# A feature-major final norm for 704 of 1056 tokens, a re-dealt tail, and three empty jobs behind each key block

## The chip, the core and the metric

The kernel runs as one program on one core of a Trainium2 chip. The core has five engines that run side by side, each through its own instructions in order: TensorE (PE in the profile, with its weight loads as PEld), VectorE (DVE), ScalarE (ACT), GpSimd (POOL) and SyncE (SP), which here only issues DMA transfers. ACT issues a few transfers too. Engines wait for each other through semaphores. The metric is the device time of one execution in microseconds (us); the kernel before takes 1604.93 us, the median of three runs from 1604.6 to 1605.01 us.

## What is computed

The reference is one layer of a streaming encoder, for a prompt of 1024 tokens and a sample of 32 tokens, 1024 features each, all in float32:

```
h  = rmsnorm(x, g_mix) * (1 + sc1) + sh1;   u = h @ w_in         # 8 heads of attention, 4 heads of an mLSTM, gates
ya = chunk-band softmax attention(q, k, v);  ym = mLSTM(...)
x  = x + gt1 * ((sigmoid(ga) * (ya @ w_br_att) + sigmoid(gm) * (ym @ w_br_mlstm)) @ w_out)
h2 = rmsnorm(x, g_ffn) * (1 + sc2) + sh2;   g, up = split(h2 @ w_gate_up)
x  = x + gt2 * ((silu(g) * up) @ w_down)
y  = x * rsqrt(mean(x * x over the 1024 features) + 1e-6) * g_final      # the final norm
```

Results are y for both streams, and the new keys, values, convolution rows and mLSTM states. The change touches the last line, and the order of some work near the first product.

## The kernel before

**Layout.** Prompt and sample are handled as one sequence of 1056 tokens in three tiles of 352 (`TILES`). Activations lie with features on the 128 partitions and tokens along the free dimension: `x2[j]` holds features 128 j to 128 j + 127 of all tokens, j from 0 to 7. Each float32 product is made of three matmuls of rounded operands (high by high, low by high, high by low: `PASSES`), so weights and activations are split into a high and a low part, by ACT (copy, L413) and DVE or POOL (subtraction, L414). `unit` (L447) makes one output block of 128 features by 352 tokens: 8 steps of k with three matmuls each. A product goes into a PSUM bank; the three banks of the pool `mm` go round among units and transposes, and a bank is free when ACT and DVE have taken its content.

**The order of the work.** PE, ACT, DVE and POOL run their instructions in the order in which the Python program emits them; SP's transfers are placed by the tile framework. Two queues of side work are woven in: `side.later` is a list of small jobs, of which `unit` runs one after each of the steps k = 2, 4, 6 (`side.flush(1)`, L450), and generators in `side.jobs` are advanced by `side.tick()`, one tick in two steps of k. An entry `lambda: None` in the list uses up one of these places.

**The start.** The first key block (hp = 0) and value block are computed together in `first_units`, while the input is still being normed. `k_block.run` then evicts the key block from PSUM (ACT L557 and L560, DVE L562), splits the next weights if there is room (L413, L414) and sends the keys out; `v_block.run` evicts the values (ACT L590) and appends `v_tail(0)`, nothing, `v_tail(1)`, nothing, `v_sample` and `cache_kv` to the list. `v_tail` transposes four blocks of values on PE (L615), splits them (ACT L603, DVE L606), and the second one sends them out from ACT's queue (L579, L580). Then `q_block(0)` makes three units with these jobs inside them and evicts each (ACT L643, L646). After it comes the key block of hp = 1 (`mm_868` in the rows below, with the weights `wsp_704`). The other three key blocks are followed by a value block of three units of its own, and at those places the list is empty.

**The end.** The down projection's first 704 tokens (`cut`) are finished in the tiles `cs[j]`. The last loop (from L2211) makes the product of the remaining 352 tokens: for each j, 22 steps of k with three matmuls (L2220), so 66 matmuls and 11 ticks, and adds it to `x2[j]` (DVE L2230). Beside it runs the generator `finish_some`, 15 steps in 75 ticks: eight steps that add `cs[j]` to `x2[j]` (DVE L2192), and then, for six blocks of up to 128 tokens, `Finish`: eight transposes on PE to have tokens on partitions (L2124), the sum of squares by ACT with an accumulator (L2125), three small operations on POOL for the reciprocal root (L2132 to L2134), two multiplications on DVE (L2140) and the output (SP L2144). `End` does the same for the last 352 tokens in three blocks of 128, 128 and 96: `ahead` during the last j, and `last` after it: three transposes (L2162), three squares (L2163), POOL's sum and power per block (L2179, L2180), then per block ACT scales the left half (L2183), DVE the right one (L2184), and ACT's and SP's queues send them (L2188). The block of 96 lies across the end of the prompt, so each of its halves goes out as two transfers.

## Time and profile before

One execution was profiled. Its own time was 1605.1 us, its span, from the first instruction to the last, 1603.4 us; the medians of the runs and this execution agree within 0.2 us. The granted TensorE clock was 0.997 of full speed on the mean.

| what | number |
|---|---|
| median of three runs | 1604.93 us |
| profiled execution: its own time / its span | 1605.1 / 1603.4 us |
| busy: PE, DVE, ACT, POOL | 1574.2, 1133.5, 784.1, 443.0 us |
| idle PE behind one wait in the first 110 us, the longest after the input load | 3.1 us |
| DMA: moved, mean rate | 192.45 MB, 120 GB/s |

How to read it: a group or a row of the timeline gives start, duration, engine, line, operation, output<-inputs, shape and count, and in brackets how long the engine had been idle and what ended it. `PE mm L615 <- ACT t L590: 3.1, 1, 3.1` in a view of waits is: TensorE's instructions of line 615 waited for ACT's of line 590, 3.1 us in total, once, at most 3.1 us. The chain of waits follows the work that ended last back through the program, and gives what each piece added to it.

### The profile page before, as it was taken

The numbers are of one execution on the slowest core, as the hardware profiler recorded it, in microseconds if no ns is written. First come the engines' busy times: TensorE is split into PE (matmuls) and PEld (weight loads), VectorE is DVE, ScalarE is ACT, GpSimd is POOL, SyncE is SP. The second block draws the span as 40 slices with busy tenths as digits, with TensorE's granted clock in tenths as the row PEclk, the third lists the DMA queues.
The fourth block names the chain that finished last, engine by engine and source line by source line (L and its number), as shares of the span: only waits on it lengthen the run. The fifth ranks groups of instructions, "written<-read, shape, count | busy, mean of one in ns | idle before, by whom it ended". The sixth has DMA issues, their size and how long they took to land.

```text
span 1603.4 us, 27301 instructions
## 1 busy us (share of the span) xinstructions
PE 1574.2 (98%) x10229; PEld 1554.3 (97%) x10229; DVE 1133.5 (71%) x2178; ACT 784.1 (49%) x1743; POOL 443.0 (28%) x470
## 2 busy tenths in 40 slices
PE   7899999999999999999999999999999999999997
PEld 7899999999999999999999999999999999999997
DVE  7766564647776855455654699998888986799754
ACT  3556454544455544443443655544544444545443
POOL 1334243434332411000012100565565650000001
PEclk9999999999999999999999999999999999999999
DMA  9822323232223332685353311213222227427454
GB/s 364 262 83 91 100 82 102 89 122 87 67 80 80 72 94 68 120 279 165 122 154 112 107 54 50 97 56 104 81 80 94 67 84 251 135 79 250 135 155 127
DMA packets 209362, 192.45 MB, mean 120 GB/s; under 512 B 11450, under 2 KB 179038, under 8 KB 208206
## 3 DMA queue, kind: packets, MB, share of 16 engines
q1 hardware_dynamic: 206670, 188.87, 37.9%
q8 instruction: 81, 1.33, 0.4%
q10 hardware_dynamic: 2528, 1.77, 0.4%
q14 instruction: 51, 0.42, 0.1%
q0 software_dynamic: 32, 0.06, 0.0%
HBM read 152.19 MB, written 41.63 MB: 121 GB/s over the span
## 4 chain that ended last, share of the span: by engine, by line
PE 89%; DMA 4%; DVE 3%; ACT 2%; issue 1%; SPq 0%; POOL 0%; ACTq 0%; DVEq 0%; POOLq 0%
PE mm L447 41%; PE psb L1817 18%; PE mm L1817 10%; PE mm L2220 3%; PE mm L884 3%; PE psb L2220 2%; PE psV L786 2%; PE psb L2063 2%; DMA xres<-s 1%; PE psS L728 1%; DMA s<-in_w_ada_dram 1%; PE psT L755 1%; PE mm L2063 1%; DMA wraw<-in_w_in_dram 1%; DMA s<-in_x_prompt_dram 1%
## 5 line engine op out<-in xcount | busy, mean ns | idle before, releaser
L447 PE MATMUL mm<-s,wsp 128*128 128x352 f32 x4104 | 687.8, 324 | 0.0
L447 PEld LDWEIGHTS mm<-s,wsp 128*128 128x128 f32 x4104 | 657.1, 188 | 1.5 <-issue 0.4
L414 DVE TENSOR_TENSOR wsp<-wraw,wsp 128x512 fp32r<-128x512 f32 (+1 forms) x280 | 234.9, 855 | 120.3 <-ACT wsp L413 118.7
L1817 PE MATMUL psb<-s,wsp 128*128 128x352 f32 x1611 | 271.7, 322 | 1.5 <-DVE wsp L414 0.8
L413 ACT ACTIVATE wsp<-wraw 128x512 fp32r<-128x512 f32 x336 | 199.4, 617 | 140.7 <-PE psb L1817 45.5
L1817 PEld LDWEIGHTS psb<-s,wsp 128*128 128x128 f32 x1611 | 260.5, 188 | 2.1 <-DVE wsp L414 1.1
L1817 PE MATMUL mm<-s,wsp 128*128 128x352 f32 x933 | 159.3, 322 | 0.0
L1817 PEld LDWEIGHTS mm<-s,wsp 128*128 128x128 f32 x933 | 151.2, 188 | 0.5 <-DVE wsp L414 0.5
L748 POOL TENSOR_SCALAR st<-st,mx 128x640 f32<-128x640 f32 (+5 forms) x72 | 56.1, 779 | 182.6 <-DVE mx L747 168.3
L1207 DVE SCALAR_TENSOR_TENSOR t<-wa,cmix,t 128x512 f32<-128x512 f32 x112 | 89.8, 807 | 14.3 <-DMA wa<-in_w_ada_dram 14.0
L414 POOL TENSOR_TENSOR wsp<-wraw,wsp 128x512 fp32r<-128x512 f32 x56 | 75.1, 1362 | 50.8 <-ACT wsp L413 50.3
L743 ACT ACTIVATE st<-st,mx 128x640 f32<-128x640 f32 (+5 forms) x72 | 47.9, 665 | 67.3 <-DVE mx L742 67.2
L742 DVE CUSTOM_DVE_ANT_0 st<-psS,bias 128x640 f32<-128x640 f32 (+5 forms) x72 | 44.4, 617 | 49.4 <-PE psS L728 35.2
L762 ACT ACTIVATE pT<-psT 128x640 fp32r<-128x640 f32 (+3 forms) x80 | 38.7, 494 | 64.6 <-PE psT L755 51.2
L1764 POOL TENSOR_TENSOR t<-t,sl 128x352 f32<-128x352 f32 x19 | 18.4, 969 | 182.9 <-ACT sl L1762 182.9
L2132 POOL TENSOR_TENSOR fst<-fst 128x1 f32<-128x1 f32 (+1 forms) x6 | 1.2, 194 | 236.6 <-ACT t L2125 236.6
L767 DVE TENSOR_TENSOR pT<-psT,pT 128x640 fp32r<-128x640 f32 (+3 forms) x80 | 44.0, 558 | 22.3 <-ACT pT L762 22.2
L1426 POOL TENSOR_TENSOR wraw<-wraw,raw 128x512 f32<-128x512 f32 x33 | 55.8, 1704 | 0.9
L884 PE MATMUL mm<-s,s 128*128 128x264 f32 (+3 forms) x432 | 54.7, 283 | 0.0
L2220 PE MATMUL mm<-s,wsp 128*128 128x352 f32 x330 | 54.4, 324 | 0.0
L2220 PEld LDWEIGHTS mm<-s,wsp 128*128 128x128 f32 x330 | 53.1, 188 | 0.0
L1426 POOL TENSOR_TENSOR spare<-wraw 128x512 f32<-128x512 f32 x11 | 16.8, 1527 | 130.0 <-DMA wraw<-in_w_gate_up_dram 122.2
(374 smaller groups left out, 2548.0 us busy)
## 6 DMA issues: line engine op xcount, KB each, us to landing
wraw<-in_w_in_dram SPq DMA_DIRECT2D x38, 512.0 KB, 4.3
wraw<-in_w_gate_up_dram SPq DMA_DIRECT2D x33, 512.0 KB, 4.0
wa<-in_w_ada_dram SPq DMA_DIRECT2D x64, 256.0 KB, 2.8
wraw<-in_w_down_dram SPq DMA_DIRECT2D x32, 512.0 KB, 3.7
a_d<-t SPq DMA_DIRECT2D x22, 528.0 KB, 2.7
g_d<-t SPq DMA_DIRECT2D x16, 528.0 KB, 2.7
x<-xres SPq DMA_DIRECT2D x16, 528.0 KB, 6.5
t<-g_d SPq DMA_DIRECT2D x16, 528.0 KB, 4.6
```

The source lines that it names most:

```text
L413: act.activation(dst[:, 0], src, AF.Copy)
L414: eng.tensor_tensor(dst[:, 1], src, f(dst[:, 0]), op=ALU.subtract)
L447: pe.matmul(pt[:, :hi - lo], wt[(w0 + k) // 4][:, a, (w0 + k) % 4], xt[k][:, b, lo:hi], start=(k == 0 and q == 0), stop=(k == n - 1 and q ...
L742: dve.tensor_tensor_reduce(so, sv, bi, -1.0, 3.0e38, ALU.add, ALU.min, mx[:n, 1:2])
L743: act.activation(st[:n, :w], st[:n, :w], AF.Exp, bias=mx[:n, 1:2], scale=-1.0, accum_out=mx[:n, 2:3])
L748: pool.tensor_scalar(st[:n, :w], st[:n, :w], mx[:n, 3:4], 1.0, op0=ALU.mult, op1=ALU.mult)
L884: pe.matmul(pt[:n, :wd], hs[k][:, a, i * P:i * P + n], whl[b][:, k, :wd], start=(k == 0 and q == 0), stop=(k == KD - 1 and q == 2))
L1207: dve.scalar_tensor_tensor(ac[:, c], wa, cmix[:, c, k:k + 1], ac[:, c], op0=ALU.mult, op1=ALU.add)
L1426: self.eng.tensor_tensor(a(dst), a(x), a(y), op=op)
L1817: pe.matmul(acc, wt[:, a, k], x[k][:, b], start=(start and not onto and k == 0 and q == 0), stop=(stop and k == 3 and q == 2), skip_group_ ...
L2063: pe.matmul(acc, wt[k // 4][:, u, k % 4], piece_of[k, i][:, v], start=(k == 0 and q == 0), stop=(k == KP - 1 and q == 2))
L2220: pe.matmul(acc, wt[(k - k0) // 4][:, u, (k - k0) % 4], piece_of[k, 2][:, v], start=(k == 0 and q == 0), stop=(k == NF - 1 and q == 2))
```

## The change

Line numbers of the changed kernel differ by one from L566 on, and by more from L2107 on.

1. `k_block` appends three empty jobs to `side.later`.
2. `finish_some` no longer transposes. Each of its first eight steps adds `cs[j]` to `x2[j]`, squares it on ACT into a tile of 128 by 704, and adds it on POOL to a running tile `known`. After one empty step, six matmuls with a column of ones sum `known` over the partitions into one PSUM tile of 128 by 8, DVE scales it and POOL takes the power for all tokens in one instruction; after three steps more the reciprocal roots are broadcast over the partitions (`bcast_cols`: six transposes on PE, two copies on ACT), and eight steps multiply `x2[j]` in place by `g_final` (a column per j, `gcols`) and by the roots, and send it out. The generator runs with 22 steps in 66 ticks after a delay of 8.
3. The outputs are `y_rows`, feature-major, for the 704 tokens, and `y_end`, token-major, for the rest; the host puts them together without arithmetic.
4. `End.last` takes sum and power of blocks 1 and 2 in one instruction each; ACT scales the left halves of blocks 0 and 1, POOL that of block 2, DVE the three right halves; six transfers follow, four from SP's queue and two from ACT's.

```diff
             sp.dma_start(new_k_p[hp], kf[:, :512])
             sp.dma_start(new_k_s[hp], kf[:, 512:])
+            side.later += [lambda: None] * 3
...
-    class Finish:
...
         def last(self):
             self.take(KD - 1, KD, 2)
             st = self.st
-            for i in range(3):
-                pool.tensor_tensor(st[:, 0, i:i + 1], st[:, 0, i:i + 1], st[:, 2, i:i + 1], op=ALU.add)
-                pool.tensor_tensor(st[:, 3, i:i + 1], st[:, 0, i:i + 1], mhalf[:, 0:1], op=ALU.pow)
-            for i, (y, py, (a, b)) in enumerate(zip(self.ys, self.py, self.cuts)):
-                n, r = b - a, st[:b - a, 3, i:i + 1]
-                act.activation(y[:n, :512], y[:n, :512], AF.Copy, scale=r)
-                dve.scalar_tensor_tensor(y[:n, 512:], py[1][:n], r, gB[:n, 512:], op0=ALU.mult, op1=ALU.mult)
-                for eng, cs in ((act, slice(0, 512)), (sp, slice(512, D))):
-                    for q, u, v in col_segments(a, b):
-                        out = y_sample[0, u - S:v - S] if q else y_prompt[0, u:v]
-                        eng.dma_start(out[:, cs], y[u - a:v - a, cs])
-
-    def finish_some(ranges):
+            for i in (slice(0, 1), slice(1, 3)):
+                pool.tensor_tensor(st[:, 0, i], st[:, 0, i], st[:, 2, i], op=ALU.add)
+                pool.tensor_tensor(st[:, 3, i], st[:, 0, i], mhalf[:, i], op=ALU.pow)
...
+            for i, (y, py, r, n, _) in enumerate(items):
+                if i < 2:
+                    act.activation(y[:n, left], y[:n, left], AF.Copy, scale=r)
+                else:
+                    pool.tensor_scalar(y[:n, left], y[:n, left], r, 1.0, op0=ALU.mult, op1=ALU.mult)
+                dve.scalar_tensor_tensor(y[:n, right], py[:n], r, gB[:n, right], op0=ALU.mult, op1=ALU.mult)
+            put(0, left)
+            put(0, right)
+            put(2, left)
+            put(1, left, act)
+            put(1, right)
+            put(2, right, act)
+
+    def finish_some():
+        known, rb = tmpt(), tmpt()
         for j in range(KD):
-            dve.scalar_tensor_tensor(x2[j][:, :cut], cs[j], gt2[:, 0, j:j + 1], x2[j][:, :cut],
-                                     op0=ALU.mult, op1=ALU.add)
+            x = x2[j][:, :cut]
+            dve.scalar_tensor_tensor(x, cs[j], gt2[:, 0, j:j + 1], x, op0=ALU.mult, op1=ALU.add)
+            if j == 0:
+                act.activation(known[:, :cut], x, AF.Square)
+            else:
+                sq = tmpt()
+                act.activation(sq[:, :cut], x, AF.Square)
+                pool.tensor_tensor(known[:, :cut], known[:, :cut], sq[:, :cut], op=ALU.add)
             yield
-        last = None
-        for a, b in ranges:
-            x = Finish(a, b)
-            x.take(0, KD)
-            x.scale()
-            if last:
-                last.put()
-            last = x
+        yield
+        pt = bank(8)
...
+        for i, (a, b) in enumerate(subs):
+            pe.matmul(pt[:b - a, i:i + 1], known[:, a:b], ones[:, 0:1], start=True, stop=True)
...
+        pool.tensor_tensor(rs[:, 1], rs[:, 0], mhalf[:, :8], op=ALU.pow)
+        for _ in range(3):
             yield
-        last.put()
+        bcast_cols(rb, rs[:, 1], [b - a for a, b in subs], 0)
+        yield
+        for j in range(KD):
+            x = x2[j][:, :cut]
+            dve.scalar_tensor_tensor(x, x, gcols[:, j:j + 1], rb[:, :cut], op0=ALU.mult, op1=ALU.mult)
+            sp.dma_start(y_rows[j], x)
+            yield
...
-    job = side.start(finish_some([(a, min(a + P, cut)) for a in range(0, cut, P)]), 15, 75)
+    gcols = sl_pool[0].tile([P, KD], F32, tag="gcols", name="gcols", bufs=1)
+    sp.dma_start(gcols, g_cols)
+    job = side.start(finish_some(), 22, 66, 8)
```

What it moves, at the three places that matter below.

**The queries of heads 0 and 1, on PE** (`mm_...` are PSUM tiles, `t_714` the evicted values, `s_...` with three matmuls a row are one step of k). Before:

```order
L447 MATMUL mm_729<-s_520,s_637 128x352 x3
L615 MATMUL mm_740<-ident,t_714 128x128 x4
L447 MATMUL mm_729<-s_547,s_637 128x352 x3
L447 MATMUL mm_729<-s_574,s_637 128x352 x3
L447 MATMUL mm_729<-s_600,s_637 128x352 x3
L447 MATMUL mm_729<-s_627,s_637 128x352 x3
L615 MATMUL mm_759<-ident,t_714 128x128 x4
L447 MATMUL mm_729<-s_664,s_637 128x352 x3
L447 MATMUL mm_779<-s_438,s_637 128x352 x3
```

and now:

```order
L447 MATMUL mm_729<-s_664,s_637 128x352 x3
L447 MATMUL mm_761<-s_438,s_637 128x352 x3
L447 MATMUL mm_761<-s_486,s_637 128x352 x3
L447 MATMUL mm_761<-s_520,s_637 128x352 x3
L616 MATMUL mm_772<-ident,t_714 128x128 x4
L447 MATMUL mm_761<-s_547,s_637 128x352 x3
L447 MATMUL mm_761<-s_574,s_637 128x352 x3
L447 MATMUL mm_761<-s_600,s_637 128x352 x3
L447 MATMUL mm_761<-s_627,s_637 128x352 x3
L616 MATMUL mm_791<-ident,t_714 128x128 x4
L447 MATMUL mm_761<-s_664,s_637 128x352 x3
L447 MATMUL mm_811<-s_438,s_637 128x352 x3
```

The first query unit (`mm_729`) runs through, and the value transposes stand in the second unit, one unit or 24 matmuls later; the other three key blocks leave PE's order as it was.

**The same place on ACT,** with the semaphores that an instruction waits for in brackets (a name with DMAHW is a transfer's). Before:

```order
L590 ACTIVATE t_714<-psT_272 128x352 [waits PE_49]
L603 ACTIVATE s_739<-mm_740 128x8x64 [waits DVE_49,PE_49,Pool_49]
L603 ACTIVATE s_739<-mm_759 128x8x64 [waits PE_49]
L579 ACTIVATE stg_766<-mm_759 128x512 [waits DVE_49]
L580 DMA out_dram<-stg_766 128x4x128 [waits DMAHW6_49,Activation_49]
L643 ACTIVATE t_723<-mm_729 128x352 [waits PE_49]
```

and now:

```order
L591 ACTIVATE t_714<-psT_272 128x352 [waits PE_49]
L644 ACTIVATE t_723<-mm_729 128x352 [waits PE_49]
L647 ACTIVATE s_722<-mm_729 64x352 [waits DVE_49,Pool_49]
L604 ACTIVATE s_771<-mm_772 128x8x64 [waits DMAHW0_49,PE_49]
L604 ACTIVATE s_771<-mm_791 128x8x64 [waits PE_49]
L580 ACTIVATE stg_798<-mm_791 128x512 [waits DVE_49]
L581 DMA out_dram<-stg_798 128x4x128 [waits DMAHW6_49,Activation_49]
L644 ACTIVATE t_723<-mm_761 128x352 [waits PE_49]
```

The first unit is evicted ahead of the value tail, the second one (`mm_761`) behind it and behind its transfer (L581).

**The last loop, on PE** (`psb_...` and `mm_...` are PSUM tiles, `x_1802` to `x_1805` the tiles of `x2`). The start of the first token block before:

```order
L2220 MATMUL psb_16344<-s_9663,wsp_16316 128x352 x3
L2124 MATMUL psb_16359<-ident,x_1802_14095 128x128
L2124 MATMUL psb_16359<-ident,x_1803_14096 128x128
L2124 MATMUL psb_16359<-ident,x_1804_14097 128x128
L2124 MATMUL psb_16359<-ident,x_1805_14098 128x128
L2124 MATMUL psb_16360<-ident,x_1802_14095 128x128
```

and the two places that stand for all six blocks now:

```order
L2212 MATMUL mm_16277<-s_10104,wsp_16278 128x352 x3
L2182 MATMUL psb_16330<-ones,t_16074 128x1 x5
L2182 MATMUL psb_16330<-ones,t_16074 64x1
L2212 MATMUL mm_16277<-s_10104,wsp_16279 128x352 x6
...
L2212 MATMUL psb_16382<-s_10229,wsp_16355 128x352 x3
L246 MATMUL mm_16415<-ident,fst_16331 128x128 x4
L246 MATMUL mm_16421<-ident,fst_16331 128x128
L246 MATMUL mm_16421<-ident,fst_16331 128x64
```

48 transposes are gone; six matmuls of one column and six transposes of the roots have come.

More of the change, by code (lines that the diff above doesn't have):

```diff
@@ L2258 @@
             a = _np.concatenate([_np.asarray(inputs[n]).reshape(-1, P) for n in _PARAMS]).T
+        elif name == "g_cols":
+            a = _np.asarray(inputs["g_final"]).reshape(KD, P).T
         else:
@@ L2280 @@
         outs[i] = _np.ascontiguousarray(outs[i].transpose(1, 2, 0)).reshape(1, 1, 3, D)
+    rows, end = outs[:2]
+    y = _np.concatenate([rows.reshape(D, 2 * NT).T, end])
+    outs[:2] = [_np.ascontiguousarray(y[None, :S]), _np.ascontiguousarray(y[None, S:])]
     return tuple(outs)
```

52 lines of the change are left out of this document (16 added, 36 removed).

## The prediction

> **What bounds the kernel now.** I read the page first, then TensorE's waits, then the timeline around the longest of them, then the chain of waits at the end. On the page:
>
> ```profile
> PE 1574.2 (98%) x10229; PEld 1554.3 (97%) x10229; DVE 1133.5 (71%) x2178; ACT 784.1 (49%) x1743; POOL 443.0 (28%) x470
> PE 89%; DMA 4%; DVE 3%; ACT 2%; issue 1%; SPq 0%; POOL 0%; ACTq 0%; DVEq 0%; POOLq 0%
> ```
>
> TensorE bounds nearly everything, so a change pays in three ways only: TensorE gets less to do, waits less, or the work after its last matmul gets shorter. This change has one part of each kind. The view of TensorE's waits shows the two that matter:
>
> ```profile
> PE mm L615 <- ACT t L590: 3.1, 1, 3.1
> PE psT L755 <- POOL wsp L414: 1.5, 1, 1.5
> ```
>
> The first lies where the empty jobs act. Its timeline (start, duration, engine and line):
>
> ```profile
> 68.37 1.69 PE L447 MATMUL mm<-s,s 128*128 128x352 f32 x9
> 71.56 1.15 ACT L413 ACTIVATE wsp<-wraw 128x512 fp32r<-128x512 f32 x2 [1.89 <-DMA wraw<-in_w_in_dram]
> 72.61 0.80 ACT L590 ACTIVATE t<-psS 128x352 f32<-128x352 f32 x2
> 73.11 1.12 PE L615 MATMUL mm<-ident,t 128*128 128x128 f32 x4 [3.06 <-ACT t L590]
> 73.88 3.11 PE L447 MATMUL mm<-s,s 128*128 128x352 f32 x12
> 76.31 0.42 SPq L674 DMA_DIRECT2D t<-in_cache_v_dram  x1
> 78.81 0.60 ACT L579 ACTIVATE stg<-mm 128x512 f32<-128x512 f32 x1 [0.76 <-DVE s L606]
> 80.24 0.44 ACTq L580 DMA_DIRECT2D out_dram<-stg  x1
> 80.73 0.46 ACT L643 ACTIVATE t<-mm 128x352 f32<-128x352 f32 x1 [1.32 <-PE mm L571]
> 81.09 0.93 ACT L646 ACTIVATE s<-mm 64x352 fp32r<-64x352 f32 x2
> 82.07 2.19 PE L447 MATMUL mm<-s,s 128*128 128x352 f32 x12 [0.16 <-ACT s L646]
> ```
>
> ACT stood behind a weight transfer (L413, 71.56), could not evict the values, and TensorE stood at their transposes from 70.05 to 73.11. The 12 matmuls behind them took 3.11 us, and the windows say why:
>
> ```profile
> 70.05:73.10 3.05, 0.00 (x1) 0.00 (x0) 0.69 (x2) 1.54 (x4) 0.84 (x1) 0.91 0.97 268
> 73.10:77.17 4.07, 4.06 (x20) 3.98 (x21) 0.69 (x1) 1.26 (x3) 3.61 (x4) 0.65 0.38 98
> 100.00:105.00 5.00, 3.53 (x22) 3.18 (x22) 3.56 (x7) 3.09 (x7) 3.56 (x3) 1.00 0.16 56
> ```
>
> The granted clock (third column from the right) fell to 0.65 on the mean after the idle 3.05 us; after the idle 1.5 us near 104 it stayed at 1.00. At 0.65 of the speed, 4.07 us hold 2.65 us of work: the stall costs 3.06 + 1.42 = 4.5 us of TensorE's time.
>
> **The empty jobs.** The value transposes move back by 24 matmuls. TensorE's step is read from the last loop's chain of waits, which also carries the second part:
>
> ```profile
> 1511.90 31.82 PE mm L2220 x198
> 1544.69 0.87 PE psb L2124 x8
> 1573.17 0.87 PE mm L2124 x8
> ```
>
> 31.82 / 198 = 0.161 us a matmul. From 68.37, the first unit ends at 72.2, and nine matmuls later, at 73.7, the transposes come: the two evictions that they need end at 73.41 (72.61 + 0.80). So the stall goes. What is late next? Three query units are 72 matmuls, 11.6 us; with nine transposes, at most 0.11 us each by the chain (0.87 / 8), 12.6 us: TensorE could begin the key block of hp = 1 at 80.95, against 86.02 before. But its PSUM bank is that of the second query unit, which ACT now evicts behind the value tail and its transfer. That transfer went out at 80.24 though its data were ready at 79.41 (78.81 + 0.60): by the order it waits for DMAHW6, the semaphore of SP's `cache_v` load issued at 76.31, and neither that load nor what stands ahead of it on SP has moved. So ACT comes to the second unit at about 80.73 as it did to the first, its two copies end at 82.02, and the key block starts at 82.07. I take that over 80.95, since the row is of the same instruction behind the same load. The remaining idle, 1.1 us, is under the 1.5 us that left the clock at 1.00. Who waits later:
>
> ```profile
> 86.02 5.94 PE L447 MATMUL mm<-s,wsp 128*128 128x352 f32 x36
> 86.55 2.50 DVE L627 TENSOR_TENSOR s<-t,s 64x352 fp32r<-64x352 f32 x4
> 89.09 1.41 DVE L1205 TENSOR_SCALAR t<-wa,cmix 128x512 f32<-128x512 f32 x1
> 91.02 1.06 DVE L562 TENSOR_TENSOR s<-mm,s 64x352 fp32r<-64x352 f32 x2 [0.52 <-ACT s L557]
> 93.94 0.40 PE L728 MATMUL psS<-s,s 128*128 128x256 f32 x2
> ```
>
> 86.02 - 82.07 = 3.95 us of gain on TensorE. DVE's splits of the cached keys and values cannot start earlier, but two of the four subtractions of L627 have gone ahead (1.25 us), and its 0.52 us of idling goes: L562 ends at about 90.3 instead of 92.08, and the bias of the first score, behind it, at 90.6. The second score (93.94 - 3.95 = 90.0) needs that PSUM tile, so TensorE stands there for 0.6 us, or less where L1205 runs shorter; I take 0.45. **Early part: -3.5 us**; ends: 0 (the stall returns in full elsewhere) and -5.05 (no pin: 86.02 - 80.95).
>
> **The norm of 704 tokens.** Six token blocks cost 6 x 0.87 = 5.22 us on the chain (first and last of six rows above). In their place come six matmuls with ones and six transposes. The second norm in the same kernel does both, and its chains give:
>
> ```profile
> 845.27 0.51 PE psV L1587 x6
> 862.30 0.30 PE mm L246 x3
> ```
>
> 0.51 + 2 x 0.30 = 1.11 us, so **-4.1 us**, if no new wait comes. Ends: -3.5 (each newcomer at 0.14 us) and -4.7 (half of it hidden). The rest of the edit is on engines with room in this loop:
>
> ```profile
> L1764 POOL TENSOR_TENSOR t<-t,sl 128x352 f32<-128x352 f32 x19 | 18.4, 969 | 182.9 <-ACT sl L1762 182.9
> L1426 POOL TENSOR_TENSOR raw<-wraw,wraw 128x512 f32<-128x512 f32 x11 | 20.0, 1817 | 0.9
> L2192 DVE SCALAR_TENSOR_TENSOR x<-s,amod,x 128x704 f32<-128x704 f32 x8 | 7.6, 946 | 0.0
> L2140 DVE SCALAR_TENSOR_TENSOR t<-psb,fst,t 128x512 f32<-128x512 f32 x8 | 5.6, 743 | 0.0
> L413 ACT ACTIVATE wsp<-wraw 128x512 fp32r<-128x512 f32 x40 | 25.1, 632 | 31.4 <-PE mm L2220 15.9 <-PE psb L2220 7.2 <-PE psb L1817 4.0
> L414 DVE TENSOR_TENSOR wsp<-wraw,wsp 128x512 fp32r<-128x512 f32 x40 | 26.7, 688 | 22.0 <-ACT wsp L413 22.0
> ```
>
> POOL's seven additions of 128 by 704 are each two of 969 ns: 1.9 us, or 2.5 us by the slowest row (1817 x 704 / 512). The generator steps every three ticks, 18 matmuls or 2.9 us, so POOL keeps up. The eighth step falls on tick 32; its product (0.95 us by L2192), square (632 x 704 / 512 = 0.87 us) and addition end about 3.9 us later, while the ones matmuls come six ticks, 5.8 us, behind it: cover 1.9 us. ACT and DVE each lose at most 1.8 us to a product and a square ahead of a weight split, but they idle 31.4 and 22.0 us in this loop waiting for tiles to come free, and weights are split a block of eight k ahead, 24 matmuls or 3.9 us. The power and DVE's scaling have nine ticks. Eight products of 946 ns replace twelve of 743 on DVE. On SP eight output transfers and one load of 4 KB replace twelve outputs; the weight loads behind them wait for DVE anyway:
>
> ```profile
> SPq L423 <- DVE wsp L414: 64.8, 21, 3.9
> ```
>
> One rule speaks against the adds. The Trainium skill, GPSIMD Engine Reference, section Engine selection, sends elementwise adds to VectorE, since GpSimd needs about twice the time for two inputs, and its Key points name contention with VectorE's two-input instructions. By its 4497 ns for 2048 elements an addition here would be an estimated 1.55 us, and the sum above would not change. The trace bears the contention out in part: over the whole kernel the same subtraction of DVE is slower than in this loop, where POOL is nearly idle:
>
> ```profile
> L414 DVE TENSOR_TENSOR wsp<-wraw,wsp 128x512 fp32r<-128x512 f32 x264 | 228.9, 882 | 113.3 <-ACT wsp L413 111.7
> ```
>
> 882 against 688 ns, on some 13 us of additions, is under 4 us of DVE's time (28%) inside its idle 22.0 us: nothing on TensorE.
>
> **The tail.** After the last product, sum and power run as before for block 0. The rows that end the kernel:
>
> ```profile
> 1596.13 2.32 DVE L2184 SCALAR_TENSOR_TENSOR t<-psb,est,t 128x512 f32<-128x512 f32 x3 [1.63 <-POOL est L2180]
> 1599.31 1.19 ACTq L2188 DMA_DIRECT2D out_dram<-t  x2
> 1598.00:1599.00 1.00, 0.00 (x0) 0.00 (x0) 0.44 (x1) 0.52 (x2) 0.00 (x0) 0.64 1.04 391
> 1601.00:1602.00 1.00, 0.00 (x0) 0.00 (x0) 0.00 (x0) 0.00 (x0) 0.00 (x0) 0.50 0.77 242
> ```
>
> The last transfer was issued until 1600.50; now it can go when DVE's third product ends, 1598.45, and is out by 1598.9: by issue 1.6 us earlier. But the 16 DMA engines were full from about 1597.7 (1.04 of their time, 391 GB/s), and the first transfer can't start earlier. 352 tokens of 4 KB are 1.44 MB; at 391 GB/s they take 3.7 us, to 1601.4, where the engines before ended at about 1601.8 (0.77 of that us). I take the bytes: **-0.45 us**; ends 0 and -1.6.
>
> **Sum:** -3.5 - 4.1 - 0.45 = -8.05 us on the profiled execution's 1605.1 (span 1603.4 and 1.7 around it), 1597.05; the median of the runs lies 0.17 lower, so **1596.9 us**.
>
> **The rivals.**
> *The early gain is given back.* Scores, cache splits and weights near 82 to 105 us hang on DVE and POOL, which gain less than TensorE; the 1.5 us at L755 shows that they are near the limit. Against it: TensorE waits for nothing longer than that wait up to the end. Without the -3.5: 1600.4.
> *No pin.* If ACT's transfer is not held by the load, the key block starts at 80.95, 1.1 us sooner, and the 0.45 us may go too: 1595.3. For it: the profile itself names L571, not a transfer, behind ACT's 1.32 us. Against: the transposes of L571 release nothing that L643 reads.
> *POOL's additions become the bound, slower than before.* The seven additions are one chain that must end before the ones matmuls. From the second step's square at about 1517 to the matmuls at 1538 there are 21 us: 3.0 us an addition is free, each 0.1 beyond costs TensorE 0.7 us. From 4.15 us the whole gain is gone; at 4.5 the stall of 10.5 us, with half speed for a while as at 73 (1.4 us), gives 1596.9 + 11.9 = 1608.8. The GPSIMD page's rule on elementwise adds would be this rival's. The rows, 1.9 to 2.5 us, speak against it.
>
> **How the numbers follow.** The forecast, 1596 to 1598.2, has 0.70; the early gain given back, wholly or in its larger part, 0.14; no pin, 0.10; POOL's chain, 0.03; the rest, 0.03, lies between. All lower ends together (-5.05 - 4.7 - 0.6) give 1594.6; the upper ones without the early gain (-3.5, tail 0.5 at most) 1601. So 1594.8 to 1600.6 leaves out under 2 in 10. 0.2%, 3.2 us, is about what a measurement here tells from no change, so faster means under 1601.7: the first three cases and half of the rest, 0.95; the same 0.02; slower 0.03.
>
> **What would show it.** Right: no wait at L616; ACT's L644 for `mm_761` at about 80.7 with the key block of hp = 1 at 82.1; a last loop without eight-fold transposes and without a wait at L2182; the final transfers' engines idle from about 1593. Wrong: a wait of TensorE for POOL at L2182, a clock below 1.00 near 80 or in the last loop, waits at L729 or L756 that were not there, or a key block that starts at 81.

## The result, and the profile after

The changed kernel is slower: 1608.62 us, the median of eight runs (1606.94 to 1612.25), against 1604.51 us before (1604.23 to 1605.31; eight runs too, of which the 1604.93 above is the median of the first three). The ratio is 1.0026, with a 95% interval from 1.0016 to 1.0035. I had forecast 1596.9 us and a range up to 1600.6. The profiled execution is the longest of the eight: 1612.25 us, with a span of 1610.5.

Its page looks like the one before. TensorE is busy for 98% of the span, and its chain only moves by two points:

```profile
PE 1576.4 (98%) x10199; PEld 1554.2 (97%) x10199; DVE 1142.2 (71%) x2177; ACT 781.0 (48%) x1728; POOL 448.7 (28%) x459
PE 87%; DMA 4%; DVE 4%; ACT 2%; issue 2%; SPq 0%; POOL 0%; DVEq 0%; ACTq 0%; POOLq 0%
```

There are 30 matmul records fewer, and yet 2.2 us more of busy TensorE: some matmuls ran slower. The view of TensorE's waits says what is new:

```profile
PE mm L2212 <- DVE wsp L414: 3.8, 5, 1.4
PE psS L729 <- DVE mx L743: 1.5, 1, 1.5
PE mm L2212 <- ACT wsp L413: 0.7, 2, 0.4
```

The stall at the value transposes (3.1 us) is gone. In its place TensorE waits 1.5 us at the second score, and in the last loop 4.5 us for weight splits, for which it did not wait at all before. There is no wait at L2182: the sum of squares was ready when the ones matmuls came. The windows of the loop (length, then busy time and count for PE, PEld, DVE, ACT and POOL, the granted clock, DMA share, GB/s) show the second cost:

```profile
1512.00:1516.00 4.00, 4.00 (x27) 4.00 (x26) 2.62 (x4) 2.41 (x4) 1.32 (x1) 1.00 0.44 131
1532.00:1536.00 4.00, 2.98 (x17) 2.45 (x16) 2.56 (x4) 2.63 (x4) 2.80 (x2) 1.00 0.37 104
1540.00:1544.00 4.00, 2.58 (x12) 2.35 (x12) 3.15 (x5) 1.09 (x3) 1.04 (x1) 0.82 0.22 61
1548.00:1552.00 4.00, 4.00 (x15) 4.00 (x15) 0.69 (x1) 0.63 (x1) 1.14 (x2) 0.50 0.00 0
```

TensorE idles for parts of every window from 1520 to 1544, and then works at half clock for about 10 us. In the profiled execution that is as dear as the waits.

**Where the 7.1 us of span went.** The start to the first value unit took 0.37 us longer, before anything that the change touches. The early part gained 2.2 us on the timeline (third transposition of the scores at 103.10 us, against 104.92):

```profile
103.10 0.52 PE L756 MATMUL psT<-ident,st 128*128 128x128 f32 x3 [1.47 <-POOL wsp L414]
```

The last loop, measured from VectorE's first addition of a finished product to its last, took 81.74 us before and now takes 90.11. Two rows of before, then two of the change:

```profile
1512.05 0.70 DVE L2230 SCALAR_TENSOR_TENSOR x<-psb,amod,x 128x320 f32<-128x320 f32 x2
1593.78 0.71 DVE L2230 SCALAR_TENSOR_TENSOR x<-mm,amod,x 128x320 f32<-128x320 f32 x2 [3.76 <-PE mm L2220]
```

```profile
1510.14 0.71 DVE L2222 SCALAR_TENSOR_TENSOR x<-psb,amod,x 128x320 f32<-128x320 f32 x2 [0.67 <-PE psb L2212]
1600.24 0.71 DVE L2222 SCALAR_TENSOR_TENSOR x<-psb,amod,x 128x320 f32<-128x320 f32 x2 [3.76 <-PE psb L2212]
```

That is 8.4 us lost where I had forecast 4.1 us gained. About half of the 8.4 us is the half clock of this execution: e2_norm, below, has the same waits at full clock, and its loop takes 85.49 us. The tail, from there to the end of the span, took 10.3 us against 9.6.

**What stretches the loop.** Here is one step of the new generator in the timeline (start, duration, engine and line):

```profile
1517.20 0.94 DVE L2167 SCALAR_TENSOR_TENSOR x<-s,amod,x 128x704 f32<-128x704 f32 x1
1518.17 0.79 ACT L2172 ACTIVATE t<-x 128x704 f32<-128x704 f32 x1 [2.74 <-DVE x L2167]
1518.87 1.14 ACT L413 ACTIVATE wsp<-wraw 128x512 fp32r<-128x512 f32 x2
1519.11 1.72 POOL L2173 TENSOR_TENSOR t<-t,t 128x704 f32<-128x704 f32 x1 [2.72 <-ACT t L2172]
1519.52 2.46 DVE L414 TENSOR_TENSOR wsp<-wraw,wsp 128x512 fp32r<-128x512 f32 x2 [1.38 <-ACT wsp L413]
1521.43 4.13 PE L2212 MATMUL mm<-s,wsp 128*128 128x352 f32 x24 [0.56 <-DVE wsp L414]
1521.90 0.94 DVE L2167 SCALAR_TENSOR_TENSOR x<-s,amod,x 128x704 f32<-128x704 f32 x1
```

Read it as a circle. VectorE's product of step j ends, ScalarE squares it, and only then come ScalarE's two weight copies, which stand behind the square in its queue. VectorE's subtractions wait for the copies. The next product stands behind the subtractions. The circle takes 4.70 us (1517.20 to 1521.90) and makes weights for 24 matmuls, which TensorE eats in 3.9. And one link in it is swollen: the two subtractions take 2.46 us, where two took 1.28 before. The first of them begins 0.41 us after GpSimd's addition, which runs until 1520.83, and ends at 1521.38.

This is not a slowdown by some per cent; the subtraction stands still until GpSimd is done. In the trace of **before**, of VectorE's 368 subtractions of 128 by 512, 102 began while a GpSimd instruction of more than 0.7 us was running. They took up to 1.79 us, and all but one of them ended between 0.543 and 0.553 us behind the end of that instruction, whenever they had begun. The 266 others took 0.67 to 0.70 us. The view of line 414 in the trace of before shows both kinds in one row (least, median and largest duration in ns; the least is of a shorter form, 128 by 256, which the row counts too):

```profile
L414 DVE TENSOR_TENSOR wsp<-wraw,wsp x280: 417/691/1791, 579.6 to 1589.6; 128x512 fp32r<-128x512 f32 x140
```

A median of 691 and a largest of 1791: I had read this group by its mean of 882 ns (the form of 512 columns) and called it 28%. The Trainium skill, SBUF — State Buffer, section Who interferes with whom, states the rule: the shared port pair is the only thing that makes engines interfere, "and it's an exclusive lock"; the page adds that it is held for the whole instruction, and that a VectorE instruction with two SBUF inputs needs it against a GpSimd instruction that reads SBUF. The 0.55 us behind GpSimd's end are what the trace has of it. I had taken only the word "contention", which stands elsewhere in the Trainium skill.

Not all of VectorE's work stands still. In the trace of before it also makes 180 additions and subtractions of 128 by 352 with one operand in PSUM (L1855). Of these, 111 began beside an addition of GpSimd, and all 180 took 0.503 to 0.523 us. The largest group of them:

```profile
L1855 DVE TENSOR_TENSOR t<-t,psb x77: 505/508/523, 978.6 to 1323.3; 128x352 f32<-128x352 f32 x77
```

### The profile page after: what moved, and what is told of

The parts are those of the page before. It is cut to its first block, busy times and chain, and to the rows that moved or that the text cites. A ratio compares the mean times of both kernels' runs of the same rounds, so it can differ in the third digit from the quotient of the medians.

```text
span 1610.5 us, 27218 instructions
## 1 busy us (share of the span) xinstructions
PE 1576.4 (98%) x10199; PEld 1554.2 (97%) x10199; DVE 1142.2 (71%) x2177; ACT 781.0 (48%) x1728; POOL 448.7 (28%) x459
## 4 chain that ended last, share of the span: by engine, by line
PE 87%; DMA 4%; DVE 4%; ACT 2%; issue 2%; SPq 0%; POOL 0%; DVEq 0%; ACTq 0%; POOLq 0%
PE mm L447 40%; PE psb L1818 18%; PE mm L1818 10%; PE psb L2212 3%; PE mm L885 3%; PE psV L787 2%; PE psb L2064 2%; PE psS L729 1%; DMA xres<-s 1%; DMA s<-in_w_ada_dram 1%; PE psT L756 1%; PE mm L2064 1%; PE mm L2212 1%; DVE wsp L414 1%; DMA wraw<-in_w_in_dram 1%
## 5 line engine op out<-in xcount | busy, mean ns | idle before, releaser
L447 PE MATMUL mm<-s,wsp 128*128 128x352 f32 x4104 | 687.9, 324 | 0.4 <-ACT s L647 0.4
L447 PEld LDWEIGHTS mm<-s,wsp 128*128 128x128 f32 x4104 | 657.0, 188 | 2.2 <-ACT s L647 0.7
L414 DVE TENSOR_TENSOR wsp<-wraw,wsp 128x512 fp32r<-128x512 f32 (+1 forms) x280 | 241.4, 880 | 117.5 <-ACT wsp L413 114.5
L1818 PE MATMUL psb<-s,wsp 128*128 128x352 f32 x1611 | 271.7, 322 | 1.6 <-DVE wsp L414 0.9
L413 ACT ACTIVATE wsp<-wraw 128x512 fp32r<-128x512 f32 x336 | 198.7, 616 | 141.1 <-PE psb L1818 46.3
L1818 PEld LDWEIGHTS psb<-s,wsp 128*128 128x128 f32 x1611 | 260.5, 188 | 2.1 <-DVE wsp L414 1.1
L1818 PE MATMUL mm<-s,wsp 128*128 128x352 f32 x933 | 159.3, 322 | 0.0
L1818 PEld LDWEIGHTS mm<-s,wsp 128*128 128x128 f32 x933 | 151.2, 188 | 0.5 <-DVE wsp L414 0.5
L414 POOL TENSOR_TENSOR wsp<-wraw,wsp 128x512 fp32r<-128x512 f32 x56 | 75.1, 1362 | 50.3 <-ACT wsp L413 49.8
L2173 POOL TENSOR_TENSOR t<-t,t 128x704 f32<-128x704 f32 x7 | 12.2, 1750 | 198.7 <-ACT t L2172 198.6
L768 DVE TENSOR_TENSOR pT<-psT,pT 128x640 fp32r<-128x640 f32 (+3 forms) x80 | 44.0, 558 | 22.6 <-ACT pT L763 22.5
L2212 PE MATMUL psb<-s,wsp 128*128 128x352 f32 x330 | 53.9, 323 | 0.0
L2212 PEld LDWEIGHTS psb<-s,wsp 128*128 128x128 f32 x330 | 53.1, 188 | 0.1
```

The lines of the kernel that those rows point to most:

```text
L413: act.activation(dst[:, 0], src, AF.Copy)
L414: eng.tensor_tensor(dst[:, 1], src, f(dst[:, 0]), op=ALU.subtract)
L447: pe.matmul(pt[:, :hi - lo], wt[(w0 + k) // 4][:, a, (w0 + k) % 4], xt[k][:, b, lo:hi], start=(k == 0 and q == 0), stop=(k == n - 1 and q ...
L1818: pe.matmul(acc, wt[:, a, k], x[k][:, b], start=(start and not onto and k == 0 and q == 0), stop=(stop and k == 3 and q == 2), skip_group_ ...
L2212: pe.matmul(acc, wt[(k - k0) // 4][:, u, (k - k0) % 4], piece_of[k, 2][:, v], start=(k == 0 and q == 0), stop=(k == NF - 1 and q == 2))
```

## The experiments

All times are medians, each beside runs of the kernel before on the same chip (1604.4 to 1604.6 us). "The loop" is the last loop measured as above, in the profiled execution.

**e1_jobs, e2_norm, e3_tail: the three parts apart.** e1_jobs adds one line to the kernel before:

```diff
+            side.later += [lambda: None] * 3
```

> The kernel before with the three empty jobs alone. The changed kernel's trace has the key block of the second pair at 81.95 us instead of 86.02, but its second score then waits 1.45 us for VectorE, and at 104 us it stands 1.8 us ahead of before, of which 0.4 us came back by 1500 us. If that is all that the jobs do: 1.3 to 2.2 us faster than before, about 1602.7. If my full early sum holds once the rest of the change is away: 3.5 us faster, 1601.0. If the early gain is given back altogether: 1604.5.

e2_norm is the change without that line and with the old order of the tail:

```diff
-            side.later += [lambda: None] * 3
...
-            for i in (slice(0, 1), slice(1, 3)):
...
+            for i in range(3):
...
+                for eng, cs in ((act, slice(0, 512)), (sp, slice(512, D))):
+                    eng.dma_start(y_end[a - cut:b - cut, cs], y[:n, cs])
```

> The change without the three empty jobs and with the old order of the tail (ScalarE scales all left halves, powers one by one, transfers from both queues), so the norm of 704 tokens alone. If the loss sits in the norm by itself: the last loop takes as long as in the changed kernel (100.4 us against 92.65) and the time is 1.3 to 2.2 us above the changed kernel's, about 1610. If the loss needs the shifted early part (another phase of weights and transfers): 1600.4, the 4.1 us that I forecast for the norm.

e3_tail is the kernel before with the new `End.last` (as in the change's diff) and the outputs `y_rows` and `y_end`; `Finish` keeps its transposes and writes its token blocks into `y_rows`:

```diff
-                    sp.dma_start(out[:, cs], y[u - self.a:v - self.a, cs])
+                sp.dma_start(y_rows[self.a:self.b, cs], y[:n, cs])
...
-            for i in range(3):
...
+            for i in (slice(0, 1), slice(1, 3)):
```

> The kernel before with the tail alone (powers of blocks 1 and 2 in one instruction, GpSimd scales one left half, six transfers into one output). My forecast: 0.45 us faster, 1604.1. By the changed kernel's trace, where the part from VectorE's last addition to the end of the span took 10.26 us against 9.62 before: 0.6 us slower, 1605.1.

Measured: e1_jobs 1602.73 us (ratio 0.9988, 0.9979 to 0.9997), e2_norm 1609.55 (1.0027, 1.0016 to 1.0038), e3_tail 1605.58 (1.0006, 0.9997 to 1.0014, so not told from no change). Against 1604.62 that is -1.9, +4.9 and +1.0 us, together +4.0; the whole change has +4.1. The parts add up, closer than such times could promise, since each interval is about 1.4 us or more to either side. The loss is the norm's, without any help from the early shift. In e2_norm's profiled execution the loop takes 85.49 us at full clock, 3.8 us more than before; the 100.4 and 92.65 us of its expectation count the loop from its first matmul.

**e4_noadd: without GpSimd's additions.**

```diff
                 act.activation(sq[:, :cut], x, AF.Square)
-                pool.tensor_tensor(known[:, :cut], known[:, :cut], sq[:, :cut], op=ALU.add)
```

> The change without GpSimd's seven additions of 128 by 704 (the sum of squares then holds the first block alone, so y is scaled wrongly; all else runs). Theory lock: VectorE's two-input subtraction cannot run beside GpSimd's addition but stands until it ends, and this is what stretches the step to 4.75 us. Then without the additions a step costs at most 3.5 us for 24 matmuls' 3.9 us, TensorE waits under 0.5 us in the loop, its clock stays at full speed, and the time is 1598 to 1600. Rival order: the loop through VectorE's product, ScalarE's square, the weight copies behind the square and the subtractions behind the copies is enough by itself. Then TensorE still waits 2 us or more in the loop and the time stays at 1603 or above.

Measured: 1600.24 us (ratio 0.9972, 0.9961 to 0.9982), 8.4 us less than the change. TensorE waits for no weight in the loop, which takes 78.95 us. The same step, from its timeline:

```profile
1518.12 1.29 DVE L414 TENSOR_TENSOR wsp<-wraw,wsp 128x512 fp32r<-128x512 f32 x2 [1.38 <-ACT wsp L413]
1519.34 0.94 DVE L2167 SCALAR_TENSOR_TENSOR x<-s,amod,x 128x704 f32<-128x704 f32 x1
1520.37 0.80 ACT L2172 ACTIVATE t<-x 128x704 f32<-128x704 f32 x1 [1.76 <-DVE x L2167]
1521.72 1.29 DVE L414 TENSOR_TENSOR wsp<-wraw,wsp 128x512 fp32r<-128x512 f32 x2 [0.57 <-ACT wsp L413]
1522.93 0.94 DVE L2167 SCALAR_TENSOR_TENSOR x<-s,amod,x 128x704 f32<-128x704 f32 x1
```

The circle is still there (VectorE still waits for ScalarE, ScalarE for the product), but it takes 3.59 us, and the two subtractions 1.29. The rival that product, square and copies are enough by themselves falls. The time and the step lie a little above what I had expected (1600 us and 3.5 us at most).

Between e2_norm and this run the loop differs by 6.5 us, while e2_norm's view shows 4.5 us of waits for weights. A wait costs more than the idle time in the view: a matmul's row lasts 0.32 us, while the next matmul of an unbroken row begins 0.161 us after it. By the starts of the matmuls the seven waits of e2_norm cost 5.8 us; 0.7 us are not placed.

**e5_dve, e6_late, e7_split: three ways to take the lock or the circle apart.** In e5_dve VectorE makes the additions, one step late:

```diff
+            if held is not None:
+                dve.tensor_tensor(known[:, :cut], known[:, :cut], held[:, :cut], op=ALU.add)
...
-                pool.tensor_tensor(known[:, :cut], known[:, :cut], sq[:, :cut], op=ALU.add)
```

> The changed kernel with the seven additions on VectorE, each one step late (behind the next product, while ScalarE squares), so GpSimd is idle in the loop. Theory lock: VectorE loses 0.87 us a step instead of 1.2, at a place where it waits for ScalarE's copies anyway; a step stays under 3.9 us, and the time is that without additions, 1600.2, up to 1601.5. If it is not the lock but the mere presence of seven more instructions of 128 by 704 on the chain: 1606 or more.

In e6_late GpSimd keeps them, but square and addition of step j - 1 are issued ahead of the product of step j:

```diff
+            if j:
+                square(j - 1)
             dve.scalar_tensor_tensor(x, cs[j], gt2[:, 0, j:j + 1], x, op0=ALU.mult, op1=ALU.add)
```

> The changed kernel with GpSimd's additions kept, but each square and its addition issued one step later, ahead of the next product, so that ScalarE's weight copies no longer stand behind a square that waits for the product just made. If the stretched step needs both the lock and the loop through product, square, copy and subtraction: the loop is cut, VectorE has 0.87 for the product, 0.9 for the subtractions and at most 1.2 us of blocked time in a step of 2.9 us, so TensorE waits under 1.5 us in all and the time is 1600.2 to 1602.5. If the lock alone sets the step, whatever the order: 1606 or more.

In e7_split each addition is cut into four:

```diff
-                pool.tensor_tensor(known[:, :cut], known[:, :cut], sq[:, :cut], op=ALU.add)
+                for c in range(0, cut, cut // 4):
+                    pool.tensor_tensor(known[:, c:c + cut // 4], known[:, c:c + cut // 4], sq[:, c:c + cut // 4], op=ALU.add)
```

> The changed kernel with each of GpSimd's additions cut into four of 128 by 176. If GpSimd holds the way to the tile memory for a whole instruction and lets VectorE in between two: a subtraction loses one piece, 0.45 to 0.6 us, instead of up to 1.2; the step comes down from 4.75 to 4.1 to 4.4 us, and the time to 1603 to 1606. If both engines only share a rate (no lock): VectorE loses the same in sum and the time stays at 1607 to 1610, or more for four starts.

Measured: e5_dve 1600.49 us (ratio 0.9975, 0.9965 to 0.9985; loop 79.11), e6_late 1601.27 (0.9980, 0.9971 to 0.9989; loop 79.58), e7_split 1604.99 (1.0003, 0.9995 to 1.0012; loop 83.49). e5_dve says that the same arithmetic costs nothing when VectorE does it. e6_late is the more telling one, since the lock stays in full:

```profile
1521.88 2.17 POOL L2172 TENSOR_TENSOR t<-t,t 128x704 f32<-128x704 f32 x1 [0.55 <-ACT t L2171]
1522.40 2.40 DVE L2178 SCALAR_TENSOR_TENSOR x<-s,amod,x 128x704 f32<-128x704 f32 x1
1524.28 0.42 ACT L413 ACTIVATE wsp<-wraw 128x256 fp32r<-128x256 f32 x1 [1.31 <-PE mm L2218]
```

Here it is the product that stands 1.5 us behind GpSimd (2.40 instead of 0.94 us), and GpSimd itself takes 2.17 instead of 1.72. But ScalarE's next copy waits for TensorE to give a tile back, not for the product: the splits are ahead again, and TensorE waits for none. So it takes both, the lock and the circle; either one alone leaves the norm a gain. In e7_split the lock goes back and forth within a step:

```profile
1518.62 3.70 POOL L2174 TENSOR_TENSOR t<-t,t 128x176 f32<-128x176 f32 x4 [0.54 <-ACT t L2172]
1519.03 1.69 DVE L414 TENSOR_TENSOR wsp<-wraw,wsp 128x512 fp32r<-128x512 f32 x2 [1.38 <-ACT wsp L413]
1520.64 1.25 DVE L2167 SCALAR_TENSOR_TENSOR x<-s,amod,x 128x704 f32<-128x704 f32 x1
```

VectorE's two subtractions come down from 2.46 to 1.69 us, while GpSimd's four pieces take 3.70 us for what one instruction did in 1.72. The lock is given back between instructions, to either side.

**e8_best: a candidate.** Empty jobs, old tail, squares one step late on ScalarE, additions two steps late on VectorE, all against the change (`add` is VectorE's addition of a square to `known`):

```diff
+            if j:
+                sqs.append(square(j - 1))
             dve.scalar_tensor_tensor(x, cs[j], gt2[:, 0, j:j + 1], x, op0=ALU.mult, op1=ALU.add)
+            if j > 2:
+                add(sqs[j - 2])
             yield
```

> A candidate: the three empty jobs, the tail as before, and the norm with squares one step late on ScalarE and additions two steps late on VectorE, so no engine waits for a product just made and GpSimd adds nothing. From the single parts: 1600.24 (no additions) less the 0.96 us that the new tail cost: 1599.3; range 1598.5 to 1600.5. If VectorE's seven additions of 0.95 us bring stalls back: 1601 to 1603.

Measured: 1600.02 us (ratio 0.9972, 0.9962 to 0.9982), loop 78.81. Near the upper end of what was expected, and 0.5 us under e5_dve.

**e9_memset, e10_unpin, e11_dvesub: the early wait.** The early part gained 1.9 us instead of 3.5. In the changed kernel's timeline the same lock stands there, GpSimd's weight subtractions ahead of VectorE's work for the score:

```profile
85.67 2.99 POOL L414 TENSOR_TENSOR wsp<-wraw,wsp 128x512 fp32r<-128x512 f32 x2 [0.17 <-POOL s L649]
85.82 1.70 DVE L607 TENSOR_TENSOR s<-t,s 128x512 fp32r<-128x512 f32 x1
87.44 2.16 DVE L628 TENSOR_TENSOR s<-t,s 64x352 fp32r<-64x352 f32 x2
91.59 0.51 PE L729 MATMUL psS<-s,s 128*128 128x256 f32 x2 [1.45 <-DVE mx L743]
```

The three runs start from e8_best. e9_memset replaces the two subtractions, for this one weight (L413 and L414's second pair on GpSimd), by memsets:

```diff
+                eng = pool if (W.done or home is slots) and not hm_n[1] else dve
+                turns[0] += eng is pool and home is not slots
+                if turns[0] in (3, 4) and eng is pool and home is not slots:
+                    act.activation(t[:, 0, :n], raw[:, 4 * i:4 * i + n], AF.Copy)
+                    pool.memset(f(t[:, 1, :n]), 0.0)
+                    continue
+                split_to(t[:, :, :n], raw[:, 4 * i:4 * i + n], eng)
```

> The candidate with GpSimd's subtractions for the second weight of the down-copied stream (two of 128 by 512 beside the first scores, 85.7 to 88.7 us in the changed kernel) replaced by two memsets of the same tiles, so these weights have no low part and the outputs that hang on them lose accuracy; nothing else changes. Theory lock: VectorE's subtractions of the cached values and queries beside it (1.70 and 2.16 us in the changed kernel) come down to 0.69 and 1.25 us, its next work starts 1.5 to 1.9 us sooner, and TensorE's wait at the second score, 1.4 us, falls to under 0.45: 1.0 to 1.4 us faster than the candidate, 1598.8. If the memset holds VectorE as an addition does: no difference, 1600.0. If the wait has another cause: VectorE's two instructions shorten but the wait stays.

e10_unpin puts off the transfer in `put_tokens`, for the first pair of heads, to the end of the list of side jobs:

```diff
-        act.dma_start(out[0, 0].rearrange("(i p) h d -> p i (h d)", p=P)[:, :, hp * P:(hp + 1) * P], stg)
+        go = lambda: act.dma_start(
+            out[0, 0].rearrange("(i p) h d -> p i (h d)", p=P)[:, :, hp * P:(hp + 1) * P], stg)
+        side.later.append(go) if hp == 0 else go()
```

> The candidate with the first values' transfer from ScalarE's queue put off behind the query units, so that ScalarE does not stand at it waiting for the cache load. My forecast's pin: the second query unit is then evicted as soon as TensorE is done with it, the key block of the second pair starts at 80.9 to 81.2 us instead of 81.95, but TensorE waits as much longer at the second score, since VectorE sets that: the time stays within 0.3 us of the candidate, 1600.0. If VectorE's chain moves along too: 1.0 us faster, 1599.0. If the pin was not the transfer: the key block still starts at 81.95.

e11_dvesub gives these two subtractions to VectorE:

```diff
+                if turns[0] in (3, 4):
+                    eng = dve
```

> The candidate with those two subtractions on VectorE instead of GpSimd (complete and exact). Theory lock: VectorE takes 1.4 us more of its own, but its neighbours lose the 1.9 us of standing; TensorE's wait at the second score shrinks by 0.2 to 0.6 us: 1599.4 to 1599.8. Without a lock VectorE would have 1.4 us more to do ahead of the score: 1601.4.

Measured, against 1600.02: e9_memset 1599.05 us, e10_unpin 1599.07, e11_dvesub 1599.49 (ratios to before 0.9967, 0.9966 and 0.9969, each about 0.0012 either way). They ran on another chip than e8_best, on which the kernel before took 1604.41 us instead of 1604.56, and the runs of e8_best (1599.23 to 1600.99) overlap with those of e9_memset (1598.44 to 1599.71) and e11_dvesub (1599.06 to 1599.59). So the argument rests on the waits in the traces, and the times agree with it. In e9_memset, VectorE's rows beside the memset, and the score:

```profile
85.37 1.26 POOL L441 MEMSET wsp<- 128x512 f32 x2
86.20 0.69 DVE L615 TENSOR_TENSOR s<-t,s 128x512 fp32r<-128x512 f32 x1
86.81 1.06 DVE L636 TENSOR_TENSOR s<-t,s 64x352 fp32r<-64x352 f32 x2
89.89 0.47 PE L737 MATMUL psS<-s,s 128*128 128x256 f32 x2
```

0.69 and 1.06 us instead of 1.70 and 2.16, and no wait at the score. The memset is also the shorter instruction (0.6 us against 1.5). But the subtraction at 86.20 began 0.43 us before the second memset ended, at 86.63, and took only what it takes alone: the memset did not hold it. (VectorE's cast ahead of it, at 85.11, took 1.06 us beside the memsets and 0.60 in the change; why is open.) That the wait came from GpSimd's two subtractions is shown, and about 1 us is their price. e11_dvesub agrees: with 1.3 us more of its own to do, VectorE still has the score's turn 0.9 us sooner (TensorE waits 0.55 instead of 1.45). In e10_unpin the first rows are those of the pin:

```profile
79.12 0.46 ACT L646 ACTIVATE t<-mm 128x352 f32<-128x352 f32 x1
81.53 5.94 PE L447 MATMUL mm<-s,wsp 128*128 128x352 f32 x36
90.10 0.50 PE L731 MATMUL psS<-s,s 128*128 128x256 f32 x2 [0.48 <-DVE mx L745]
```

ScalarE evicts the second query unit at 79.12 us (80.24 in e8_best), TensorE runs into the key block without a wait (0.33 us in e8_best), and the wait at the score falls to 0.48. The key block starts at 81.53, later than the 80.9 to 81.2 that I had expected, because TensorE itself is not done sooner. So the transfer was the pin. What it waits for is the landing of the cached values: their last piece landed at 80.16, 80.06 and 79.69 us in before, the change and e8_best, and ScalarE's transfer went out 0.08 us later each time. My expectation that VectorE would eat the gain was wrong: ScalarE's copies feed VectorE's chain, which moved along, and 0.95 us came out.

**e12_both: a version that beats both kernels.** e8_best with the edits of e10_unpin and e11_dvesub:

```diff
+                if turns[0] in (3, 4):
+                    eng = dve
...
+        side.later.append(go) if hp == 0 else go()
```

> The candidate with both: the first values' transfer put off, and the two subtractions on VectorE. Apart they left TensorE 0.48 and 0.55 us of its 1.45 us wait at the second score and gained 0.95 and 0.53 us. If VectorE's chain carries both: the rest of the wait goes, 1598.6 us. If the transfer's gain already held all that is to be had there: 1599.1.

Measured: 1598.11 us (1597.88 to 1598.21; ratio 0.9960, 0.9946 to 0.9974), 6.5 us under the kernel before and 10.5 under the change, and 0.5 us less than expected if both gains add up. TensorE does not wait at the second score:

```profile
89.32 0.40 PE L737 MATMUL psS<-s,s 128*128 128x256 f32 x2
```

## Why the prediction was wrong

**The early part: right in mechanism, 1.6 us too much.** The stall at L615 went, no clock was lost near 80, ScalarE came to `mm_761` behind its transfer, and the key block of hp = 1 began at 81.95 us, where I had put it at 82.07. The rival without a pin fell with it, and e10_unpin shows the pin itself. The term that was mis-sized is VectorE's friction: 0.45 us forecast, 1.45 measured. A further wait of 0.39 us, at L756 (97.76) behind VectorE's L768, I had put at nothing. A row of the friction was in my own fences: the bias of 0.47 us (L1205, 93.21 in the trace of before) had taken 1.41 us at 89.09, beside GpSimd's subtractions:

```profile
88.77 2.88 POOL L414 TENSOR_TENSOR wsp<-wraw,wsp 128x512 fp32r<-128x512 f32 x2
```

I saw that it "runs shorter" sometimes and did not ask why. Moved back in time, the same two subtractions of GpSimd met VectorE's subtractions instead, ahead of the score. e1_jobs puts the whole part at -1.9 us, between my ends of 0 and -5.05.

That 81.95 lies so near to 82.07 is in part luck. The start took 0.37 us longer and TensorE's units 0.2 us longer, the pin came 0.12 us sooner, and TensorE waited there for 0.42 us, not for the 1.1 that I had worked out. The price of the stall, too, came from a single execution: with the same code at this place, the stall at L615 was 3.06 us in before, 2.03 in e3_tail and 1.63 in e2_norm. From the first unit's start to the third transposition these three took 36.55, 36.10 and 35.09 us, and the change 34.36, so the part gained 0.7 to 2.2 us, by which of them it is compared with.

**The norm: wrong, and here the forecast broke.** The failed step is the paragraph on contention: "882 against 688 ns, on some 13 us of additions, is under 4 us of DVE's time (28%) inside its idle 22.0 us: nothing on TensorE". Two things in it were wrong. The mean of 882 ns was taken for a rate, where the group is a mixture of 0.68 us and of up to 1.79 us, depending on whether GpSimd was ahead. And the idle 22.0 us were taken for cover, with the weights split 24 matmuls ahead. They were time in which VectorE waited for ScalarE's copies, and the new square tied those copies to VectorE's own product, so that what VectorE lost to GpSimd came back to it one step later. What the runs show in its place: each subtraction stands until GpSimd's addition is done, up to 1.2 us; the step takes 4.70 us for 24 matmuls, which last 3.9; TensorE waits 4.5 us; and the loop takes 85.49 us at full clock (e2_norm), where the forecast had 4.1 us less than 81.74. An engine's idle time covers a delay only if what it waits for does not hang on that delay. e4_noadd, e5_dve and e6_late show that each half of this is needed: 1600.24, 1600.49 and 1601.27 us.

The work itself was also over-counted as a gain. Without any wait the loop is 2.8 to 2.9 us shorter (78.95 and 78.81 against 81.74), not 4.1. The chain of e4_noadd has the two newcomers:

```profile
1536.79 1.22 PE psb L2181 x12
1538.01 5.03 PE mm L2211 x30
1546.90 0.74 PE mm L246 x6
1547.65 32.02 PE psb L2211 x198
```

The six ones matmuls count as twelve records and cost 1.22 us. Their forecast rested on a misreading: the six records of 0.51 us in the earlier norm (L1587) are three such matmuls, each recorded twice, for the three token blocks of one tile, and not six. The six broadcasts cost 0.74 us, not 0.60. So 1.96 us come for 5.22 that go, which is 3.3 us of gain. The last 0.4 us are in the 462 matmuls of the product on this chain, which take 74.70 us and took 74.33 before. They are lost in the two rows behind the newcomers: 30 matmuls at 0.161 us would be 4.83 us, and 198 took 31.82.

**The rival that ended slower was the right sign for a wrong reason.** I gave 0.03 to GpSimd's chain becoming the bound at the ones matmuls, and found 1.9 to 2.5 us for an addition. An addition took 1.75 us on the mean, and no wait stood at L2182. GpSimd was quick enough; it was in the way. The Trainium skill, GPSIMD Engine Reference, section Key points, which I had quoted for "contention", names the kind of instruction that suffered, one of VectorE with two SBUF inputs.

**The tail: no gain, and rather a loss.** The time of e3_tail alone is not told from that of before. But from VectorE's last addition to the end of the span the eight kernels with the old order took 9.6 to 10.0 us, and the six with the new one 10.0 to 10.6. Issuing sooner worked: the last transfer goes out 4.7 us behind VectorE's last addition instead of 6.1. The first byte does not move, as I had argued. The step that failed is the rate that I took for fixed. Windows of e3_tail, whose last addition comes at the same time as before's (1593.76 and 1593.78); the last two columns are the DMA engines' busy share and GB/s:

```profile
1599.00:1600.00 1.00, 0.00 (x0) 0.00 (x0) 0.00 (x0) 0.00 (x0) 0.00 (x0) 0.50 1.04 307
1602.00:1603.00 1.00, 0.00 (x0) 0.00 (x0) 0.00 (x0) 0.00 (x0) 0.00 (x0) 0.50 0.12 45
```

and two of the kernel before:

```profile
1599.00:1600.00 1.00, 0.00 (x0) 0.00 (x0) 0.00 (x0) 0.28 (x1) 0.00 (x0) 0.50 1.05 395
1600.00:1601.00 1.00, 0.00 (x0) 0.00 (x0) 0.00 (x0) 0.00 (x0) 0.00 (x0) 0.50 1.03 326
```

As busy as before, the engines moved 307 GB/s in the microsecond from 1599 and not 395, and had bytes left after 1602, where before they had none. Nor was the rate fixed in the kernel before: my 391 GB/s was that of one microsecond, and two later it was 326. A packet of 2 KB, of which the last blocks make 704, took 92 ns on the mean in before and 97 in e3_tail and in the change. Over 16 engines that is 0.2 us, while the last byte came 0.8 us later behind the last addition (8.95 us against 8.16); most of the loss is that the engines were not all busy to the end (0.84 and 0.12 of the last two microseconds in e3_tail). Whether the number of transfers in flight causes this, or their queues or their order, stays open: no run varied one of these alone.

**The loop's clock, which I had left out.** The mean granted clock was 0.998 in the three runs of the change under 1608 us and 0.995 in the two above 1611; the last section shows what lies behind that.

## What to carry to other kernels

Before work goes to GpSimd, look at single instructions of VectorE with their inputs in SBUF, not at their mean: where a group shows a short duration and a spread of long ones, look at what GpSimd was doing, and price each addition there at up to its full length on VectorE's path (here up to 1.2 of 1.72 us). The bias, with one tensor and a column as inputs, stood too (1.41 instead of 0.47 us), so two-input instructions are not the only ones to look at; those with an operand in PSUM did not stand. Before idle time is counted as cover, follow what the engine waits for; a new instruction between two in-order queues can close a circle whose length then sets the pace, and issuing it one step late opens it again. A part that gains on its own (the empty jobs, 1.9 us) can hide behind one that loses, so parts are best timed apart.

## What the hardware showed that I had not expected

**The clock can fall without a long gap, and need not.** In the profiled change no wait in the loop was longer than 1.42 us, and still the clock was halved for some 10 us. e2_norm has the same waits and kept full speed. Windows of the change, then of e2_norm:

```profile
1538.00:1543.00 5.00, 3.34 (x18) 2.81 (x17) 4.18 (x7) 2.66 (x5) 1.68 (x1) 0.96 0.37 105
1543.00:1553.00 10.00, 10.00 (x40) 9.97 (x39) 1.66 (x6) 1.26 (x2) 2.09 (x2) 0.51 0.33 92
```

```profile
1538.00:1543.00 5.00, 3.34 (x18) 2.78 (x18) 4.18 (x6) 2.66 (x5) 1.68 (x1) 1.00 0.36 105
1543.00:1553.00 10.00, 10.00 (x67) 9.97 (x66) 4.08 (x11) 2.53 (x4) 2.08 (x2) 1.00 0.50 144
```

TensorE was busy for 3.34 of 5 us in both; one then made 40 matmuls in 10 us and the other 67. The loop took 90.11 and 85.49 us.

The 14 traces of this case suggest why. In each of them the granted clock changes only at times that lie a multiple of 3.41 us apart, as on a grid. A stretch at half clock lasts 3.41 us (72.52 to 75.94 in before) or three times that (1542.57 to 1552.81 in the change). In the grid's window just ahead of four such falls TensorE was busy for 0.94, 1.38, 1.62 and 1.75 of 3.41 us (before, e3_tail, e7_split, the change), about half or less; other windows of the change, with 2.40 and 2.78 us, left the clock at full speed. In e2_norm the grid lies otherwise and cuts the same dip in two, 1537.82 to 1541.23 and 1541.23 to 1544.64, with 2.68 and 2.48 us busy, and the clock stayed. So it looks as if the busy share of a fixed window counts, not the longest gap, and as if chance places the windows. This is worked out from these traces alone, and it does not fit them all: e2_norm kept its clock behind a window with 1.78 us near 70, e1_jobs behind one with 1.72 near 1590, and near 15 us the clock fell behind 2.06 us in e5_dve and e7_split.

The runs fit such a chance: those of the change lie within 5.3 us, those of before within 1.1 us.

**The lock works both ways.** GpSimd's additions took 1.72 us with VectorE waiting, but 2.17 and 2.35 us in e6_late, where VectorE's instruction was ahead of them.
